# Attention products over all 128 rows, with scores one chunk ahead, in a two-layer convolution / mLSTM kernel

## The chip, the core and the metric

The kernel runs on one core of one Trainium2 chip. The metric is the device time of one execution in microseconds (us); less is better. The engines are TensorE (PE, with its weight loads as PEld), VectorE (DVE), ScalarE (ACT), GpSimd (POOL) and SyncE (SP), which here issues the DMAs.

## The reference

Two layers of a small diffusion backbone on 1024 latent and 256 context tokens of width 1024: first a gated short convolution, then a bidirectional mLSTM with eight heads, each followed by a squared-ReLU MLP. All is float32. The change lies in the mLSTM. For a head (q and k 64 wide, v 128 wide), a direction and a chunk of 128 tokens the reference computes

```python
logd = b[..., :, None] - b[..., None, :] + ic[..., None, :]
logd = jnp.where(tri, logd, -jnp.inf)
s = jnp.einsum('bhtd,bhsd->bhts', qc, kc) * jnp.exp(logd - m_t[..., None])
num = jnp.einsum('bhts,bhsv->bhtv', s, vc) + w_inter[..., None] * jnp.einsum('bhtd,bhdv->bhtv', qc, c_mat)
den = jnp.sum(s, axis=-1) + w_inter * jnp.einsum('bhtd,bhd->bht', qc, n_vec)
out = num / jnp.maximum(jnp.abs(den), jnp.exp(-m_t))[..., None]
...
c_new = a[..., None, None] * c_mat + jnp.einsum('bhsd,bhsv->bhdv', kc * wk[..., None], vc)
```

and adds the outputs of the forward and of the backward direction. The states c_mat and n_vec at each chunk's start are carried over the chunks.

## The kernel before

The layers follow each other on the one core. In the mLSTM the heads go in four pairs (0 to 3); two heads of 64 lie one above the other in the 128 partitions. For a pair the kernel projects k, v and q (`psk`, `psv`, `psq`, products of float32r with 128 rows), then comes `states` and then `attend` for each of its two heads.

`states` transposes k chunk by chunk (`pk`), weighs it (`kk`), multiplies it with V, and puts the forward state of each of ten steps in partitions 0 to 63 of `st[hh]`, the backward one in 64 to 127 (L977 on ACT, L978 on DVE). Eight recurrences per head on DVE (L982) carry the states on.

`attend` takes eight chunks of 128 latent tokens. First `qw`: the weights w of both directions are fetched into the two halves of the partitions (L993) and multiplied with the head's q (L994). Then for each chunk c:

- `Dm`, a tile for two chunks and both directions, is fetched every second chunk (L1002), gets the triangular mask added on DVE (L1004) and is put through the exponential on ACT (L1009); three buffers.
- the scores `po` (L1011): 64 rows of kT against 64 rows of qT, those of the head;
- `pm` (L1015, DVE): the scores times both directions' exponentials;
- for each direction d a product of `pm` with V over 128 rows (L1019) and, added to it in PSUM, one of 64 rows of `qw` with 64 rows of the state (L1020). The column 128 of the 129 is the denominator; each direction has a PSUM bank of its own;
- absolute values on ACT (L1026), maximum and reciprocal on DVE (L1027, L1028), the forward output scaled on ACT (L1030), the backward one scaled and added on DVE (L1031), and the sum of squares on ACT (L1032).

The outputs `hb` of a head (four buffers) wait for `out_gate` (projection `pso`, sigmoid) and `read_out` (transposes `pth`), which stand after the next pair's psq.

The order on each engine is static. A scheduler makes it when the program is built: it follows priorities, and puts projections of the next pair (psk, psv; in pair 3 the pso of pairs 2 and 3) between the chunks. SP issues its DMAs in order too, and a DMA whose buffer is not yet free holds up those behind it.

## Time and profile before

| | us |
|---|---|
| three runs | 2639.1, 2613.77, 2613.24 |
| median of these | 2613.77 |
| profiled execution | 2626.18 |
| its span, first to last instruction | 2624.4 |

| engine | busy us | share of the span |
|---|---|---|
| PE | 2549.2 | 97% |
| DVE | 1634.4 | 62% |
| ACT | 1149.1 | 44% |
| POOL | 98.8 | 4% |

Busy time is the time in which an instruction of the engine runs. Instructions overlap, so that an engine's pace is read from the starts of successive ones, not from their lengths. A float32 product stands in the trace as two records. `64*128` in a row is rows times columns of the array that the weights fill. The granted clock is that of TensorE, as a share of 2.4 GHz.

### The profile page before, as it was taken

Reading aid. Unit: us, or ns where it says so; the run is one execution under the profiler, and the core shown is the slowest. Engines: PE = TensorE matmul, PEld = TensorE weight load, DVE = VectorE, ACT = ScalarE, POOL = GpSimd, SP = SyncE. Lnnn points to the kernel's source line nnn. Section 1 sums busy time; section 2 is a strip of 40 time slices with the busy share of each in tenths; the row PEclk is TensorE's granted clock in tenths of the full one; section 3 lists DMA queues with packets and bytes.
Section 4 is the critical chain, followed back from the end, with each engine's and each line's share of the span. In section 5 each row is a group of like instructions: output and inputs, shape, how many; then the busy total and the mean of one; then the engine's idle time right before and its main releaser. Section 6 shows DMA issues by size and latency. Waiting matters only on the chain.

```text
span 2624.4 us, 38836 instructions
## 1 busy us (share of the span) xinstructions
PE 2549.2 (97%) x14520; PEld 2227.5 (85%) x14520; DVE 1634.4 (62%) x3036; ACT 1149.1 (44%) x2545; POOL 98.8 (4%) x223
## 2 busy tenths in 40 slices
PE   8999999979999999999999999999998999999998
PEld 5888887879999998888878888787878999988887
DVE  5677885677676664455764653526567777754565
ACT  6311113555445453334654534335455555554443
POOL 1000000100000000000120000000010000000010
PEclk9999999989999999999999999979999999999999
DMA  8456653436665675556741322221435777676665
GB/s 290 129 183 191 209 178 114 147 122 228 224 231 210 221 253 169 171 155 195 232 147 53 70 70 68 61 53 37 150 108 199 260 241 261 230 254 190 184 224 189
DMA packets 229631, 452.77 MB, mean 173 GB/s; under 512 B 17738, under 2 KB 109178, under 8 KB 229442
## 3 DMA queue, kind: packets, MB, share of 16 engines
q1 hardware_dynamic: 229442, 450.29, 53.1%
q8 instruction: 114, 1.87, 0.3%
q14 instruction: 75, 0.61, 0.1%
HBM read 324.68 MB, written 125.33 MB: 171 GB/s over the span
## 4 chain that ended last, share of the span: by engine, by line
PE 54%; issue 30%; DMA 7%; DVE 6%; ACT 2%; POOL 1%; SPq 0%; DVEq 0%; POOLq 0%; ACTq 0%
PE psd L528 11%; PE op L371 5%; PE psv L853 4%; PE psZ L429 4%; PE psW L429 4%; PE psX L429 4%; PE pso L129 3%; DMA mraw<-in_mod_w_dram 3%; PE psc L129 2%; PE psY L429 2%; DMA Dm<-nm_d 2%; PE psu L129 2%; PE psb L129 2%; PE po L1020 1%; DVE macc L220 1%
## 5 line engine op out<-in xcount | busy, mean ns | idle before, releaser
L528 PE MATMUL psd<-w,hp 128*128 128x512 f32 x3024 | 705.0, 395 | 0.0
L528 PEld LDWEIGHTS psd<-w,hp 128*128 128x128 f32 x3024 | 568.9, 188 | 132.2 <-DVE p L548 0.2
L523 DVE TENSOR_TENSOR hp<-hr,hp 128x512 fp32r<-128x512 f32 (+1 forms) x226 | 169.3, 751 | 255.1 <-ACT hp L522 254.8
L522 ACT CAST hp<-hr 128x512 fp32r<-128x512 f32 (+1 forms) x226 | 151.2, 669 | 325.8 <-PE psd L528 295.6
L123 DVE TENSOR_TENSOR w<-raw,w 128x512 fp32r<-128x512 f32 x384 | 261.1, 684 | 37.2 <-ACT w L122 36.8
L122 ACT CAST w<-raw 128x512 fp32r<-128x512 f32 x384 | 236.4, 617 | 95.9 <-DMA raw<-in_w_dram 31.4
L429 PE MATMUL psX<-A,w 128*128 128x256 f32 (+1 forms) x1536 | 233.2, 300 | 5.0 <-ACT st L444 3.7
L429 PE MATMUL psZ<-A,w 128*128 128x256 f32 (+1 forms) x1536 | 230.8, 298 | 1.0 <-DVE st L448 1.0
L429 PE MATMUL psW<-A,w 128*128 128x256 f32 (+1 forms) x1536 | 228.1, 296 | 0.0
L429 PEld LDWEIGHTS psX<-A,w 128*128 128x128 f32 x1536 | 216.2, 191 | 6.4 <-ACT st L444 4.0
L429 PEld LDWEIGHTS psZ<-A,w 128*128 128x128 f32 x1536 | 215.2, 190 | 1.4 <-DVE st L448 1.4
L429 PEld LDWEIGHTS psW<-A,w 128*128 128x128 f32 x1536 | 213.2, 189 | 0.0
L371 PE MATMUL op<-w,zs 128*128 128x512 f32 x864 | 203.3, 394 | 1.7 <-ACT zs L365 1.7
L459 ACT ACTIVATE st<-st 128x256 f32<-128x256 f32 (+1 forms) x192 | 85.3, 444 | 247.7 <-DVE st L450 182.3
L371 PEld LDWEIGHTS op<-w,zs 128*128 128x128 f32 x864 | 160.9, 188 | 37.6 <-ACT zs L365 2.4
L220 DVE SCALAR_TENSOR_TENSOR macc<-mraw,sil,macc 128x1024 f32<-128x1024 f32 x112 | 140.5, 1280 | 38.7 <-DMA mraw<-in_mod_w_dram 38.4
L109 ACT CAST w<-raw 128x1024 fp32r<-128x1024 f32 (+1 forms) x73 | 75.3, 1039 | 161.2 <-PE psc L129 60.9
L853 PE MATMUL psv<-w,hT 128*128 128x256 f32 (+1 forms) x960 | 144.8, 305 | 0.9 <-ACT val L270 0.9
L853 PEld LDWEIGHTS psv<-w,hT 128*128 128x128 f32 x960 | 130.5, 201 | 7.6 <-issue 2.0
L429 PE MATMUL psY<-A,w 128*128 128x256 f32 (+1 forms) x768 | 121.7, 305 | 13.2 <-ACT w L122 11.6
L110 DVE TENSOR_TENSOR w<-raw,w 128x1024 fp32r<-128x1024 f32 (+1 forms) x73 | 87.6, 1208 | 69.3 <-ACT w L109 68.2
L429 PEld LDWEIGHTS psY<-A,w 128*128 128x128 f32 x768 | 111.3, 195 | 15.7 <-ACT w L122 12.4
(238 smaller groups left out, 3462.2 us busy)
## 6 DMA issues: line engine op xcount, KB each, us to landing
hid_d<-st SPq DMA_DIRECT2D x48, 896.0 KB, 5.3
mraw<-in_mod_w_dram SPq DMA_DIRECT2D x80, 512.0 KB, 3.9
hr<-hid_d SPq DMA_DIRECT2D x104, 320.0 KB, 4.0
raw<-in_w_dram SPq DMA_DIRECT2D x64, 512.0 KB, 4.2
rw<-in_w_dram SPq DMA_DIRECT2D x64, 512.0 KB, 5.8
raw<-t_d SPq DMA_DIRECT2D x128, 256.0 KB, 3.1
hr<-hid_d SPq DMA_DIRECT2D x122, 256.0 KB, 2.7
raw<-in_w_dram SPq DMA_DIRECT2D x96, 256.0 KB, 3.2
```

The source lines that it names most:

```text
L110: nc.vector.tensor_sub(w[1], src, w[0].bitcast(F32))
L122: nc.scalar.copy(w[:, 0], src)
L123: nc.vector.tensor_sub(w[:, 1], src, w[:, 0].bitcast(F32))
L129: nc.tensor.matmul(ps, w[a][:, k * P : (k + 1) * P], hold["hT"][:, k, b, t0 : t0 + n], start=(k == 0 and i == 0), stop=(k == KD - 1 and i ...
L220: nc.vector.scalar_tensor_tensor(ac[v], raw, s, ac[v], ALU.mult, ALU.add)
L371: nc.tensor.matmul(ps[h], zs[:, a, k, :], ws[k][b][:, h * 512 : (h + 1) * 512], start=(k == 0 and i == 0), stop=(k == KD - 1 and i == 2),)
L429: nc.tensor.matmul(ps, w[i][:, a, k * P : (k + 1) * P], A[:, PIECE[i], b, k, :], start=(first and k == 0 and j == 0), stop=(k == 3 and j = ...
L459: nc.scalar.activation(c, c, AF.Relu)
L522: nc.scalar.copy(h[:, 0], r)
L523: nc.vector.tensor_sub(h[:, 1], r, h[:, 0].bitcast(F32))
L528: nc.tensor.matmul(ps, h[:, a, o : o + P], w[:, b], start=(first and j == 0), stop=(last and j == 2))
L853: nc.tensor.matmul(ps[:, 0 : self.g], hold["hT"][:, k, a_, t * P : (t + 1) * P], self.wv[k // self.per][b_][:, k % self.per * self.g : (k ...
```

## The change

- `qz`, one tile for all pairs, takes the place of each pair's `qT`: for head 0 of the pair q stands in partitions 0 to 63 and zeros in 64 to 127, for head 1 the other way round. ACT copies each psq in two halves. The scores are then a product over all 128 rows of kT.
- `sts`, two state tiles made once, hold for each step the forward state over zeros, and beside it (index 1) zeros over the backward state. The recurrences (now L994) run over both, 258 columns instead of 129. The state product then takes all 128 rows of `qw`, the weighted q of both directions as one operand; the zeros take away the other direction.
- The zeros are written once, by memsets on POOL (L809, L810, L967, L968).
- Both directions' outputs lie in the bank of the scores (columns 128 to 385), so that one ACT instruction takes both absolute values.
- `front(c)` (Dm, exponentials, scores, pm) and `back(c)` (the other products and the output) are apart, and `front(c + 1)` is written ahead of `back(c)`.
- `Dm` and `hb` have two buffers instead of three and four; in pair 3 `hb` takes the buffers of kT and V.

```diff
@@ -803,6 +803,11 @@
         flcol = K1.tile([P, 8, 2, 8], F32, name="flcol")
         adb = K1.tile([P, HEADS, NT], F32, name="adb")
         mask = K1.tile([P, 2, P], F32, name="mask")
+
+        lower, upper = slice(0, 64), slice(64, P)
+        qz = K1.tile([P, 2, SEQ], F32, name="qz")
+        nc.gpsimd.memset(qz[upper, 0], 0.0)
+        nc.gpsimd.memset(qz[lower, 1], 0.0)
         nc.gpsimd.memset(mask, 0.0)
         NEG = -1e30
         nc.gpsimd.affine_select(mask[:, 0], mask[:, 0], pattern=[[1, P]], compare_op=ALU.is_ge, fill=NEG, base=0, channel_multiplier=-1)
@@ -830,7 +835,6 @@
                 self.j = j
                 self.kT = pr.tile([P, TOK], F32, tag="kT", name="kT")
                 self.V = pr.tile([P, NT, 2, 129], F32, tag="V", name="V")
-                self.qT = pr.tile([P, SEQ], F32, tag="qT", name="qT")
                 nc.gpsimd.memset(self.V[:, :, :, 128:129], 1.0)
                 self.g, self.per = (GP, 3) if j == 0 else (256, 4)
                 with tc.high_priority(offset=HP if j == 0 else 0):
@@ -866,7 +870,10 @@
                 for t0, n in groups:
                     ps = tp.tile([P, 512], F32, tag="tp", name="psq")
                     mm_feat(ps[:, 0:n], w, t0, n)
-                    nc.scalar.activation(self.qT[:, t0 - CTX : t0 - CTX + n], ps[:, 0:n], AF.Identity, scale=0.125)
+                    for hh, r in enumerate((lower, upper)):
+                        nc.scalar.activation(
+                            qz[r, hh, t0 - CTX : t0 - CTX + n], ps[r, 0:n], AF.Identity, scale=0.125
+                        )
 
         XG = ((256, 512), (768, 512))
         pair = Pair(0)
@@ -954,9 +961,14 @@
 
         hp = s1.enter_context(pool("head", bufs=2, side="right"))
 
+
+        sts = [hp.tile([P, NT, 2, 129], F32, name=f"st{i}", bufs=1) for i in range(2)]
+        for t in sts:
+            nc.gpsimd.memset(t[upper, :, 0], 0.0)
+            nc.gpsimd.memset(t[lower, :, 1], 0.0)
+
         def states(pair):
             j = pair.j
-            st = [hp.tile([P, NT, 129], F32, tag="st", name="st") for _ in range(2)]
             for c in range(NT):
                 pk = acc.tile([P, 512], F32, tag="acc", name="pk")
                 nc.tensor.transpose(pk[:, 0:P], pair.kT[:, c * P : (c + 1) * P], ident)
@@ -974,62 +986,76 @@
                         pk[:, o : o + 129], kk[:, hh].rearrange("p d q -> p (d q)"), pair.V[:, c, hh],
                         start=True, stop=True,
                     )
-                    nc.scalar.copy(st[hh][0:64, c], pk[0:64, o : o + 129])
-                    nc.vector.tensor_copy(st[hh][64:128, sb], pk[64:128, o : o + 129])
+                    nc.scalar.copy(sts[hh][lower, c, 0], pk[lower, o : o + 129])
+                    nc.vector.tensor_copy(sts[hh][upper, sb, 1], pk[upper, o : o + 129])
             for hh in range(2):
                 h = 2 * j + hh
                 for s_ in range(1, NT - 1):
                     nc.vector.scalar_tensor_tensor(
-                        st[hh][:, s_], st[hh][:, s_ - 1], adb[:, h, s_ : s_ + 1], st[hh][:, s_], ALU.mult, ALU.add
+                        sts[hh][:, s_], sts[hh][:, s_ - 1], adb[:, h, s_ : s_ + 1], sts[hh][:, s_], ALU.mult, ALU.add
                     )
-            return st
-
-        def attend(pair, hh, st):
+
+        def attend(pair, hh):
             h = 2 * pair.j + hh
-            pb = hh * 64
-            kT, qT, V = pair.kT, pair.qT, pair.V
+            kT, V, st = pair.kT, pair.V, sts[hh]
             qw = hp.tile([P, SEQ], F32, tag="qw", name="qw")
-            for d in range(2):
-                nc.sync.dma_start(qw[d * 64 : d * 64 + 64], w_d[d, h].partition_broadcast(64))
-                nc.vector.tensor_mul(qw[d * 64 : d * 64 + 64], qw[d * 64 : d * 64 + 64], qT[pb : pb + 64])
-            hb = hp.tile([P, 8, P], F32, tag="hb", name="hb", bufs=4)
+            for d, r in enumerate((lower, upper)):
+                nc.sync.dma_start(qw[r], w_d[d, h].partition_broadcast(64))
+                nc.vector.tensor_mul(qw[r], qw[r], qz[hh * 64 : hh * 64 + 64, hh])
+            if pair.j < HEADS // 2 - 1:
+                hb = hp.tile([P, 8, P], F32, tag="hb", name="hb")
+            else:
+                hb = pr.tile([P, 8, P], F32, tag="V" if hh else "kT", name="hb")
             ssq = small.tile([P, 8], F32, tag="ssq", name="ssq", bufs=4)
-            for c in range(8):
-                cs = slice(c * P, (c + 1) * P)
-                g = c + NCT
+            Dm = {}
+
+            def front(c):
+
                 if c % 2 == 0:
-                    Dm = hp.tile([P, 2, 2 * P], F32, tag="Dm", name="Dm", bufs=3)
-                    nc.sync.dma_start(Dm, nm_d[:, h, c * P : (c + 2) * P].partition_broadcast(P))
+                    D2 = hp.tile([P, 2, 2 * P], F32, tag="Dm", name="Dm")
+                    nc.sync.dma_start(D2, nm_d[:, h, c * P : (c + 2) * P].partition_broadcast(P))
                     for d in range(2):
                         nc.vector.tensor_add(
-                            ch(Dm[:, d]), ch(Dm[:, d]), mask[:, d].unsqueeze(1).broadcast_to([P, 2, P])
+                            ch(D2[:, d]), ch(D2[:, d]), mask[:, d].unsqueeze(1).broadcast_to([P, 2, P])
                         )
-                Dc = Dm[:, :, (c % 2) * P : (c % 2 + 1) * P]
+                    Dm[c], Dm[c + 1] = D2[:, :, 0:P], D2[:, :, P : 2 * P]
+                Dc = Dm[c]
                 for d in range(2):
                     nc.scalar.activation(Dc[:, d], Dc[:, d], AF.Exp, bias=acol[:, c, d, h : h + 1])
                 po = acc.tile([P, 512], F32, tag="acc", name="po")
+                g = c + NCT
                 nc.tensor.matmul(
-                    po[:, 0:P], kT[pb : pb + 64, g * P : (g + 1) * P], qT[pb : pb + 64, cs], start=True, stop=True
+                    po[:, 0:P], kT[:, g * P : (g + 1) * P], qz[:, hh, c * P : (c + 1) * P], start=True, stop=True
                 )
                 pm = hp.tile([P, 2, P], F32, tag="pm", name="pm")
                 nc.vector.tensor_mul(pm, po[:, 0:P].unsqueeze(1).broadcast_to([P, 2, P]), Dc)
-                o = (po[:, 128:257], acc.tile([P, 512], F32, tag="acc", name="po1")[:, 0:129])
+                return po, pm
+
+            def back(c, po, pm):
+                g = c + NCT
+                o = po[:, 128:386].rearrange("p (d v) -> p d v", d=2)
                 steps = (g - 1, NT - g)
                 for d in range(2):
-                    nc.tensor.matmul(o[d], pm[:, d], V[:, g, hh], start=True, stop=False)
+                    nc.tensor.matmul(o[:, d], pm[:, d], V[:, g, hh], start=True, stop=False)
                     nc.tensor.matmul(
-                        o[d], qw[d * 64 : d * 64 + 64, cs], st[hh][d * 64 : d * 64 + 64, steps[d]],
-                        start=False, stop=True,
+                        o[:, d], qw[:, c * P : (c + 1) * P], st[:, steps[d], d], start=False, stop=True
                     )
                 dn = small.tile([P, 2], F32, tag="dn", name="dn")
-                for d in range(2):
-                    nc.scalar.activation(dn[:, d : d + 1], o[d][:, 128:129], AF.Abs)
+                nc.scalar.activation(dn, o[:, :, 128], AF.Abs)
                 nc.vector.tensor_max(dn, dn, flcol[:, c, :, h])
                 nc.vector.reciprocal(dn, dn)
                 h1 = hp.tile([P, P], F32, tag="h1", name="h1")
-                nc.scalar.activation(h1, o[0][:, 0:P], AF.Identity, scale=dn[:, 0:1])
-                nc.vector.scalar_tensor_tensor(hb[:, c], o[1][:, 0:P], dn[:, 1:2], h1, ALU.mult, ALU.add)
+                nc.scalar.activation(h1, o[:, 0, 0:P], AF.Identity, scale=dn[:, 0:1])
+                nc.vector.scalar_tensor_tensor(hb[:, c], o[:, 1, 0:P], dn[:, 1:2], h1, ALU.mult, ALU.add)
                 nc.scalar.activation(h1, hb[:, c], AF.Square, accum_out=ssq[:, c : c + 1])
+
+            nxt_ = front(0)
+            for c in range(8):
+                cur = nxt_
+                if c < 7:
+                    nxt_ = front(c + 1)
+                back(c, *cur)
+
             def out_gate():
                 r = rstd_of(ssq, 8, 1.0 / P)
                 for i in range(0, 8, 4):
@@ -1070,8 +1096,8 @@
                 for og, ro in fin:
                     ro(og())
                 fin = []
-            st = states(pair)
-            fin += [attend(pair, hh, st) for hh in range(2)]
+            states(pair)
+            fin += [attend(pair, hh) for hh in range(2)]
         for og, ro in fin[:2]:
             ro(og())
         fin = fin[2:]
```

Two places show how the scheduled order moves. The first is TensorE in pair 1, late in its chunks; po are the chunks' products (scores L1011 before and L1027 after, with V L1019 and L1039, with the states L1020 and L1040), psv the filler. Before:

```order
L1019 MATMUL po<-V,pm 128x129
L1020 MATMUL po<-st,qw 128x129
L1019 MATMUL po_14209<-V,pm 128x129
L1020 MATMUL po_14209<-st,qw 128x129
L1011 MATMUL po<-qT,kT 128x128
L853 MATMUL psv<-w_14418,hT 128x256
L853 MATMUL psv<-w_14419,hT 128x256
L853 MATMUL psv<-w_14418,hT 128x256 x2
L853 MATMUL psv<-w_14419,hT 128x256
L1019 MATMUL po<-V,pm 128x129
L1020 MATMUL po<-st,qw 128x129
L1019 MATMUL po_14240<-V,pm 128x129
```

After:

```order
L1039 MATMUL po<-V,pm 128x129
L1040 MATMUL po<-st_12950,qw 128x129
L1039 MATMUL po<-V,pm 128x129
L1040 MATMUL po<-st_12950,qw 128x129
L1027 MATMUL po<-qz,kT 128x128 x2
L857 MATMUL psv<-w_14366,hT 128x256
L857 MATMUL psv<-w_14367,hT 128x256
L857 MATMUL psv<-w_14366,hT 128x256
L857 MATMUL psv<-w_14360,hT 128x256
L857 MATMUL psv<-w_14361,hT 128x256
L857 MATMUL psv<-w_14360,hT 128x256
L1027 MATMUL po<-qz,kT 128x128
```

Before, a chunk is four products of alternating rows, then the score of the next chunk, then some seven psv. After, the products of two or more chunks stand together, and two scores ahead of them; over a pair fewer psv stand between the chunks, and behind the last chunk stand 55, 197 and 197 psv in pairs 0 to 2 (28, 154 and 154 before) and 94 pso in pair 3 (71 before).

The second place is DVE in pair 1, with buffer numbers: each Dm is one load (Dm_14179, Dm_14230, Dm_14274, Dm_14318 follow each other before, Dm_14090, Dm_14130, Dm_14189 after), L1004 and L1018 are the masks, L1015 and L1031 the score multiplies. Before:

```order
L1015 TENSOR_TENSOR pm_14207<-po_14205,Dm_14179 128x256
L1028 RECIPROCAL dn_14194<-dn_14194 128x2
L1031 SCALAR_TENSOR_TENSOR hb_14045<-po1_14189,dn_14194,h1_14199 128x128
L1015 TENSOR_TENSOR pm_14238<-po_14236,Dm_14230 128x256
L1027 TENSOR_TENSOR dn_14214<-dn_14214,flcol_12235 128x2
L1028 RECIPROCAL dn_14214<-dn_14214 128x2
L1031 SCALAR_TENSOR_TENSOR hb_14045<-po1_14209,dn_14214,h1_14219 128x128
L1004 TENSOR_TENSOR Dm_14318<-Dm_14318,mask_12237 128x256 x2
L1027 TENSOR_TENSOR dn_14245<-dn_14245,flcol_12235 128x2
L1015 TENSOR_TENSOR pm_14258<-po_14256,Dm_14230 128x256
```

After:

```order
L1031 TENSOR_TENSOR pm_14116<-po_14114,Dm_14090 128x256
L1049 SCALAR_TENSOR_TENSOR hb_14020<-po_14074,dn_14104,h1_14108 128x128
L1031 TENSOR_TENSOR pm_14138<-po_14136,Dm_14130 128x256
L1045 TENSOR_TENSOR dn_14122<-dn_14122,flcol_12235 128x2
L1046 RECIPROCAL dn_14122<-dn_14122 128x2
L1031 TENSOR_TENSOR pm_14156<-po_14154,Dm_14130 128x256
L1049 SCALAR_TENSOR_TENSOR hb_14020<-po_14096,dn_14122,h1_14126 128x128
L1045 TENSOR_TENSOR dn_14144<-dn_14144,flcol_12235 128x2
L1046 RECIPROCAL dn_14144<-dn_14144 128x2
L1018 TENSOR_TENSOR Dm_14189<-Dm_14189,mask_12237 128x256 x2
```

Before, the load of Dm_14318 waits for pm_14207 (third load back), and its mask stands ahead of pm_14258, for which the next load waits. After, the load of Dm_14189 waits for pm_14116 (second load back), and its mask stands behind both pm of the load between, pm_14138 and pm_14156, for the second of which the following load waits.

## Rows read from the trace of the kernel before

**Rows 1.** Stretches: from:to us, length, busy us (instructions) by engine, granted clock, DMA.

```profile
1476.00:1508.00 32.00, 30.02 (x185) 23.97 (x184) 15.16 (x58) 18.75 (x82) 1.99 (x3) 1.00 0.31 62
...
1576.00:1612.00 36.00, 34.59 (x197) 27.72 (x195) 16.98 (x61) 19.59 (x87) 2.13 (x2) 0.91 0.33 70
...
1696.00:1745.00 49.00, 47.45 (x196) 38.16 (x195) 17.41 (x60) 19.58 (x86) 1.97 (x2) 0.62 0.22 54
```

**Rows 2.** Chain that ended last, in order of time: start us, us, what.

```profile
1438.81 1.26 PE pk L962 x5
...
1511.09 11.16 PE psq L129 x48
...
1546.30 0.44 PE pk L962 x4
...
1612.51 18.46 PE psv L853 x154
1630.98 11.16 PE psq L129 x48
...
1666.20 0.44 PE pk L962 x4
...
1745.59 18.47 PE psv L853 x154
...
1862.31 7.89 PE op L371 x34
```

**Rows 3.** Timeline of PE: start us, us, line, shapes; a chunk of each head.

```profile
1473.85 0.38 PE L1019 MATMUL po<-V,pm 128*128 128x129 f32 x2
...
1475.00 0.37 PE L1020 MATMUL po<-st,qw 64*128 64x129 f32 x1
1475.01 0.37 PE L1011 MATMUL po<-qT,kT 64*128 64x128 f32 x1
...
1475.42 0.39 PE L853 MATMUL psv<-w,hT 128*128 128x256 f32 x1
...
1484.79 0.38 PE L1019 MATMUL po<-V,pm 128*128 128x129 f32 x2
1485.11 0.49 PE L1020 MATMUL po<-st,qw 64*128 64x129 f32 x2
...
1486.27 0.38 PE L1011 MATMUL po<-qT,kT 64*128 64x128 f32 x2
1486.58 1.09 PE L853 MATMUL psv<-w,hT 128*128 128x256 f32 x7
```

**Rows 4.** Timeline of PE in pair 1: 128-row products beside their like.

```profile
1562.38 0.61 PE L1019 MATMUL po<-V,pm 128*128 128x129 f32 x4
1562.82 0.44 PE L973 MATMUL pk<-V,kk 128*128 128x129 f32 x2
```

**Rows 5.** Timeline of DVE, and three pieces of the chain, in pair 1.

```profile
1584.40 0.76 DVE L1004 TENSOR_TENSOR Dm<-Dm,mask 128x256 f32<-128x256 f32 x2 [1.78 <-DMA Dm<-nm_d]
...
1590.56 0.76 DVE L1004 TENSOR_TENSOR Dm<-Dm,mask 128x256 f32<-128x256 f32 x2 [1.40 <-DMA Dm<-nm_d]
...
1572.79 0.42 DVE pm L1015
...
1579.20 5.18 DMA Dm<-nm_d
```

**Rows 6.** Timeline of SP (pair 1), a group on ACT, timeline of DVE (pair 0).

```profile
1561.91 17.66 SPq L1002 DMA_DIRECT2D Dm<-nm_d  x3
...
L1009 ACT ACTIVATE Dm<-Dm,acol 128x128 f32<-128x128 f32 x24 | 8.3, 392 | 2.3 <-DVE Dm L1004 2.2
...
1462.17 2.73 DVE L982 SCALAR_TENSOR_TENSOR st<-st,adb 128x129 f32<-128x129 f32 x10
```

**Rows 7.** Timeline of POOL, and the tile qT: ns min/median/max.

```profile
1363.99 1.17 POOL L813 MEMSET gcol<- 128x1280 f32 x1 [0.85 <-DVE tt L294]
...
L869 ACT ACTIVATE qT<-psq x8: 577/594/599, 1414.0 to 1776.0; 128x512 f32<-128x512 f32 x8
```

## The prediction

> **What bounds the kernel now.** I read first the busy shares by stretch [rows 1], because the change lies only in the attention part of the mLSTM layer (1438.8 to 1862.3 us of the span; 16 chunks of scores and outputs for each of four head pairs). There TensorE is the engine that is nearly always busy: it stands still for 1.98 us of 32, 1.41 of 36 and 1.55 of 49. The reason is that projections of the next pair (psk, psv, pso) were put between the chunks as filler. Second I read the chain [rows 2]: after each pair's last chunk comes a tail of projections alone (154 psv in 18.5 us, 0.12 us each, then 48 psq in 11.2, 0.232 each). So a pair ends when TensorE has done all its work, or when the chunks' own loop is through and the tail after it.
>
> Third, the same engine's timeline [rows 3], chunk by chunk. A product of 128x129 is two records. A chunk of head 1 has five products and takes from 1484.79 to 1486.58, that is 1.79 us; one of head 0 from 1473.85 to 1475.42, 1.57 us. Where a 128-row product stands beside its like, two take 0.44 us, 0.22 each [rows 4]; alternating with 64-row ones (64\*128 in the row) they take 0.32 to 0.42. That extra is the price of the change of rows.
>
> Last, VectorE [rows 5]: the mask is added to a freshly loaded tile Dm (two chunks) at 1584.40 and 1590.56, each time after waiting 1.78 and 1.40 us for its load. A load takes 5.2 us. In DVE's order before, the mask of load k+3 stands ahead of the score multiply (pm) that frees the next buffer, so that loads follow each other one by one despite three buffers: load 5.2, mask 0.8, pm 0.4, about 6.4 us for two chunks. TensorE's 3.5 us of products plus filler just fits into that. Both bounds lie close together, and this decides the sum.
>
> A fourth thing: the clock. In pair 2 the same program as in pair 1 has a granted clock of 0.62 in the mean instead of 0.91 [rows 1], that is, long at 1.2 instead of 2.4 GHz, and from its first pk to its psv tail it takes 79.4 us instead of 66.2 [rows 2]: 13.2 us more. It fell while TensorE was working all the time on 64- and 128-row products in turn.
>
> **The change, part by part.** (a) All products take 128 rows: five products at 0.22 make 1.1 us a chunk, against a mean of 1.68 (1.57 and 1.79). That frees 0.58 x 64 = 37 us of TensorE, if nothing else moves. What I do not see is a 128-row product with half its operand zero; I take the price of the full one, 0.22 [rows 4], to which it is nearest in shape. The bounds are 0.21, what each of the two overlapping products of head 0 takes (1475.00 to 1475.42 [rows 3]), and 0.32, the cheapest product that stands beside a change of rows; at 0.32 a chunk would cost 1.6 and nothing would be gained.
>
> At one place a rule speaks against it. In head 0 the last product of a chunk and the score of the next start at 1475.00 and 1475.01 [rows 3]: they lie on different halves of the rows and run together, and head 0's chunk is 0.22 us shorter for it. The Trainium skill (TensorE: Matmul & The Clock Gate, Part 3, "The mechanism") says that small products on distinct row groups run concurrently, so that padding gives something up. The trace agrees for this neighbour pair. By that rule alone the change would lose 0.22 x 32 = 7 us; the 1.57 above already contains this overlap, and the gain of 0.58 is net of it.
>
> (b) Scores one chunk ahead, Dm with two buffers instead of three. The static order moves (order rows of the section on the change). On DVE both pm of load k+1 now stand ahead of the mask of load k+2: two loads are in flight together. One round is then load 5.2, mask 0.8, four exponentials 1.4 (0.35 each [rows 6]), pm 0.4: 7.7 us, but for two loads, four chunks: 1.9 us a chunk instead of 3.2. On TensorE the filler is packed differently: four chunks come with little between, and the psv tails grow from 154 to 197 (28 to 55 in pair 0, and in pair 3 from 71 pso to 94). So part of what TensorE gains is stood idle in the loop, waiting for loads.
>
> (c) The state recurrences on DVE now run over 258 columns instead of 129. Ten of them took 2.73 us [rows 6], 0.27 each. For 258 the bounds are 0.38 (half of the 0.76 of the two masks, 256 columns [rows 5]) and 0.54 (twice 0.27). I take 0.41, near the pm of 256 columns with its 0.42: 16 x 0.14 = 2.2 us more for each pair, in a stretch in which the first outputs wait for the last recurrence.
>
> **Pair 1, step by step.** The second pm of load 0 is done at 1561.9 (SP issues a load then [rows 6]); the states before it do not change. On DVE follow a pm, three copies (together 1.5) and 15 recurrences (6.2), then the second pm of load 1: 1569.8. The last recurrence, the first outputs with their scaling (about 3), the mask of load 3 (issued at 1569.8, landed at 1575.0), exponentials and pm bring load 2 to its second pm at about 1577.7. Two rounds of 7.7: load 6 is through at 1593.1. The last chunk's pm stands behind the mask of the next pair's first load, issued at that time: + 5.2 + 0.8 + 0.4, and four products 0.9: 1600.4. Tail 197 x 0.12 = 23.6: 1624.0, against 1631.0 now: **-7.0**. TensorE's own work would allow 1631.0 - 16 x 0.58 - 1.4 - 0.09 x 36 (the clock of 0.91) = 1617.1, so some 7 us of new idle time appear.
>
> Pair 2 has the same order: **-7.0**. Pair 0: its ten recurrences end at 1464.9 now [rows 6]; 2.2 later, with a pm, load 0 is through at 1467.5, load 2 (landed 1472.7; mask, pm, and a weighting of q, an estimate of 3 together) at about 1475.7, load 3's second pm behind load 4's mask (1481.6), in steps of 7.7 for loads 5 and 7 to 1497, output 1498, 55 psv 6.6: 1504.6 against 1511.1: **-6.5**. Pair 3: the mask of load 2 stands ahead of twelve recurrences, which stay behind its landing (issued at the first pm of head 6, by the distance in pair 0 some 20 us after that pair's start, 1795; landed 1800, then 5 for the recurrences and 2 for outputs and pm): load 2 is through only at about 1807, loads 4 and 6 at 1817 and 1827, the last outputs at 1834, then 94 pso (21.8) and 18 transposes (2.0): 1857.8 against 1862.3: **-4.5**. Sum: -25.0.
>
> (d) At nothing: the memsets of qz and of the two state tiles on POOL (each at most the 1.17 us of a larger one [rows 7]; POOL has nothing else to do there, and TensorE the psv of pair 1; without that cover the first chunk of pair 0 would come 4.7 us later). The second ACT instruction for each psq (8 x 0.6 us [rows 7]) is hidden by the 5.6 us that the next psq takes; ACT saves 64 of the 128 reads of the denominators. One output bank instead of two: ACT's first read waits for all four products, 0.4 us in a loop in which the load lasts longest. qz and the states in one copy: a pair's q is written after the last chunk before it, behind the psv tail of 18 us; without that it would wait up to one chunk.
>
> **Sum.** The profiled execution took 2626.18 us (span 2624.4 and 1.8 around it). The median of the runs, 2613.77, is 12.4 below; this is nearly the 13.2 us of the clock in pair 2. So 2626.2 - 13.2 - 25.0 = 2588.0: I predict 2588, 26 us or 1.0% below the median.
>
> **Rivals.** (1) Loads hide entirely, TensorE alone bounds: 2613 - 37 for the products - 5 to 10 for stalls and half clock now there = 2566 to 2571. For it: DMA queues are little used; against: masks standing ahead of pm in the order. (2) The clock stays at its lower level in one or two pairs, because TensorE now waits some 7 us in each: +13 each as in pair 2, 2601 with one, 2614 with two. For it: the clock fell twice in this part already [rows 1], and gaps get longer; against: products without row changes are denser, and a loop that waits for loads loses less to a slow TensorE. (3) Slower: the two buffers act as one, each load only after the last pm of the one before, 7.7 us for two chunks. Six loads after 1569.8 end at 1616.0, with output and tail 1640.5: 9.5 us more for each pair, 2613 + 38 = 2651. It decides from 6.1 us a load on, where a pair ends as now; I expect 5.0 (from 1569.8 to 1599.5 in six). Against it the order of DVE. (4) The extra on the 64-row products comes from something other than the change of rows; then the lost overlap and the longer recurrences count alone: 2613 + 7 + 4 x 2.2 = 2629. That is the rule on row groups above, taken alone.
>
> **How the numbers follow.** Main case 0.50 (own range 2576 to 2600: some 24 rounds, each up to half a microsecond longer or shorter), rival 1 0.21, rival 2 0.19, rival 3 0.06, rival 4 0.04. Range for 8 in 10: from 2564 (rival 1's lower end, less 2 to 3 for products of 0.21) to 2607, between one and two pairs at the low clock. A change of 1% (26 us) is about what a measurement can tell from none. Faster by over 1% (below 2587.6): 0.25 of the main case, all of rival 1, and 0.02 of rival 2, where the loop hides the slow clock: 0.48. Within: 0.25 + 0.17 + 0.04 = 0.46. Slower: 0.06.
>
> **What would show it.** In the profile after: products of 0.22 us without longer neighbours, about 1.1 us per chunk; DVE waiting for Dm about once per four chunks, 2 to 3 us; recurrences of 0.4; psv tails of 197 that start some 39 us after the second pm of load 0; pairs 1 and 2 some 7 us shorter than pair 1 now. The prediction is wrong if a 128-row product beside zeros costs over 0.3 us, if the mask waits come once per two chunks, or if the granted clock of the attention stretches lies below 0.8.

## The result, and the profile after

Over nine runs each the kernel takes 2593.73 us after the change (2591.92 to 2597.03) and 2616.85 before (2612.24 to 2654.64). The ratio of the means is 0.9898, with a 95% interval of 0.9872 to 0.9925; the one slow run before, 2654.64, is left out of it. The profiled execution took 2592.09 us, its span is 2590.3 (2626.18 and 2624.4 before).

The chain of waits after, in order of time (start us, us, what), answers [rows 2]:

```profile
1438.33 1.26 PE pk L974 x5
...
1506.34 11.14 PE psq L129 x48
...
1541.54 0.44 PE pk L974 x4
...
1558.80 4.87 DVE st L994 x12
...
1600.03 17.37 PE psv L857 x144
1617.40 11.15 PE psq L129 x48
...
1652.65 0.44 PE pk L974 x4
...
1704.01 23.65 PE psv L857 x197
1727.66 11.14 PE psq L129 x48
1738.80 0.66 PE pk L974 x6
...
1798.43 21.85 PE pso L129 x94
1820.29 1.32 PE pth L1077 x12
...
1825.67 1.22 DVE w L110
1826.89 1.08 DVE zs L366 x2
...
1828.01 7.00 PE op L371 x22
```

A pair lasts from its first pk to the next psq, pair 3 to op. From these rows and [rows 2] (where a psv tail ends, psq begins; pair 3 of before begins after psq, at 1745.59 + 18.47 + 11.1 = 1775.2):

| pair | before us | after us | difference | predicted |
|---|---|---|---|---|
| 0 | 72.3 | 68.0 | -4.3 | -6.5 |
| 1 | 84.7 | 75.9 | -8.8 | -7.0 |
| 2 | 97.9 | 75.0 | -22.9 | -20.2 (7.0 and 13.2 of the clock) |
| 3 | 87.1 | 89.2 | +2.1 | -4.5 |

Their sum is -33.9 of the 34.1 us by which the span is shorter; 1862.31 to the end of the span before, and 1828.01 to its end after, are both 762 us. The medians differ by 23.1 only: the profiled execution before, 9 us above its median, is one in which the clock fell in pair 2.

The stretches answer [rows 1] (from:to us, length, busy us and instructions by engine PE, PEld, DVE, ACT, POOL, granted clock, DMA):

```profile
1476.00:1506.00 30.00, 23.14 (x180) 22.33 (x179) 16.07 (x59) 17.37 (x76) 3.83 (x5) 0.94 0.41 85
1574.00:1600.00 26.00, 20.93 (x167) 19.51 (x166) 14.67 (x54) 16.16 (x73) 2.67 (x5) 1.00 0.48 114
```

The first stretch lies in pair 0, the second in pair 1. In pair 1 the clock is 1.00 where it was 0.91. But TensorE now stands still for a fifth or more of the chunk loop: 6.9 of 30 us and 5.1 of 26. What it waits for is on the timeline of PE and in its waits from 1436 to 1830 (us in total, times, longest):

```profile
1577.53 0.49 PE L1027 MATMUL po<-qz,kT 128*128 128x128 f32 x2 [1.67 <-DVE hb L1049]
```

```profile
PE po L1027 <- DVE hb L1049: 16.8, 12, 2.3
PE po L1039 <- DVE pm L1031: 5.5, 6, 1.7
PE op L371 <- ACT zs L365: 2.7, 1, 2.7
...
PE op L371 <- DVE zs L366: 2.1, 1, 2.1
```

Mostly a score waits for `hb`. It needs a PSUM bank, and a bank is free only when the output of an earlier chunk has been read out of it. That reading is late on DVE, as its timeline shows (idle time before an instruction, and what ended it, in brackets):

```profile
1575.31 0.76 DVE L1018 TENSOR_TENSOR Dm<-Dm,mask 128x256 f32<-128x256 f32 x2 [2.12 <-DMA Dm<-nm_d]
1575.99 1.22 DVE L110 TENSOR_TENSOR w<-raw,w 128x1024 fp32r<-128x1024 f32 x1
1577.12 0.35 DVE L1049 SCALAR_TENSOR_TENSOR hb<-po,dn,h 128x128 f32<-128x128 f32 x1
...
1584.33 0.76 DVE L1018 TENSOR_TENSOR Dm<-Dm,mask 128x256 f32<-128x256 f32 x2 [0.87 <-DMA Dm<-nm_d]
...
1587.88 0.76 DVE L1018 TENSOR_TENSOR Dm<-Dm,mask 128x256 f32<-128x256 f32 x2 [0.62 <-DMA Dm<-nm_d]
...
1591.42 0.42 DVE L1018 TENSOR_TENSOR Dm<-Dm,mask 128x256 f32<-128x256 f32 x1 [1.34 <-DMA Dm<-nm_d]
```

A mask waits for its load until 1575.31, and `hb` stands behind it in DVE's order, and behind a weight split of 1.22 us (L110). What `hb` reads, ACT had ready at 1574.50. Such waits for loads are not new on DVE: it had 19 of them before, 28.4 us in all, and has 23 now, 38.3 us. New is that TensorE, sooner done with its products, stands still meanwhile (rows64 below, with the slower products, hardly does). The products themselves now run at one pace (timeline of PE, pair 1; eight products, 0.22 us from start to start after the first):

```profile
1586.50 0.49 PE L1039 MATMUL po<-V,pm 128*128 128x129 f32 x2
1586.83 0.39 PE L1040 MATMUL po<-st,qw 128*128 128x129 f32 x2
...
1588.16 0.39 PE L1040 MATMUL po<-st,qw 128*128 128x129 f32 x2
1588.31 0.97 PE L857 MATMUL psv<-w,hT 128*128 128x256 f32 x6
```

### The profile page after: what moved, and what is told of

The parts are those of the page before. It is cut to its first block, busy times and chain, and to the rows that moved or that the text cites. A ratio compares the mean times of both kernels' runs of the same rounds, so it can differ in the third digit from the quotient of the medians.

```text
span 2590.3 us, 38783 instructions
## 1 busy us (share of the span) xinstructions
PE 2489.9 (96%) x14520; PEld 2202.5 (85%) x14520; DVE 1640.9 (63%) x3036; ACT 1139.0 (44%) x2489; POOL 104.8 (4%) x229
## 4 chain that ended last, share of the span: by engine, by line
PE 53%; issue 30%; DVE 7%; DMA 6%; ACT 2%; POOL 2%; SPq 0%; DVEq 0%; POOLq 0%; ACTq 0%
PE psd L528 11%; PE op L371 5%; PE psZ L429 4%; PE psW L429 4%; PE psX L429 4%; PE psv L857 3%; PE psc L129 3%; PE pso L129 3%; PE psb L129 3%; PE psu L129 3%; DMA Dm<-nm_d 3%; PE psY L429 2%; DMA mraw<-in_mod_w_dram 2%; PE psq L129 1%; POOL rstd L242 1%
## 5 line engine op out<-in xcount | busy, mean ns | idle before, releaser
L110 DVE TENSOR_TENSOR w<-raw,w 128x1024 fp32r<-128x1024 f32 (+1 forms) x73 | 87.8, 1210 | 80.1 <-ACT w L109 79.0
L857 PE MATMUL psv<-w,hT 128*128 128x256 f32 (+1 forms) x960 | 133.8, 293 | 1.1 <-ACT val L270 0.9
L857 PEld LDWEIGHTS psv<-w,hT 128*128 128x128 f32 x960 | 123.7, 192 | 1.9 <-ACT val L270 1.2
L429 PEld LDWEIGHTS psY<-A,w 128*128 128x128 f32 x768 | 111.2, 195 | 15.2 <-ACT w L122 12.4
```

Source lines behind the costliest of these rows:

```text
L110: nc.vector.tensor_sub(w[1], src, w[0].bitcast(F32))
L429: nc.tensor.matmul(ps, w[i][:, a, k * P : (k + 1) * P], A[:, PIECE[i], b, k, :], start=(first and k == 0 and j == 0), stop=(k == 3 and j = ...
L857: nc.tensor.matmul(ps[:, 0 : self.g], hold["hT"][:, k, a_, t * P : (t + 1) * P], self.wv[k // self.per][b_][:, k % self.per * self.g : (k ...
```

## The experiments

All start from the changed kernel. Its time for comparison is 2593.7 us. The kernel before, run beside each group, took 2636.5 (15 runs), 2624.1 (7), 2635.5 (7) and 2620.1 us (11) in the median, between 2609.9 and 2667.2; so each experiment's own median is compared. The changed kernel was not run again beside them, and the profiles differ outside the pairs too: the first pk starts anywhere from 1435.3 to 1442.5 us. A difference of 5 us or less counts here only where the lengths of the pairs bear it out.

**rows64: the 64-row products back.**

```diff
-                    po[:, 0:P], kT[:, g * P : (g + 1) * P], qz[:, hh, c * P : (c + 1) * P], start=True, stop=True
+                    po[:, 0:P], kT[hh * 64 : hh * 64 + 64, g * P : (g + 1) * P], qz[hh * 64 : hh * 64 + 64, hh, c * P : (c + 1) * P],
...
-                        o[:, d], qw[:, c * P : (c + 1) * P], st[:, steps[d], d], start=False, stop=True
+                        o[d], qw[d * 64 : d * 64 + 64, c * P : (c + 1) * P], st[d * 64 : d * 64 + 64, steps[d], d],
```

> The changed kernel with 64-row scores and state products again (zeros unread), outputs of the two directions in two PSUM banks; all else as changed. Theory (price of the change of rows): 0.58 us more for each of 64 chunks, 37 us of TensorE, of which the 26 us that it stands still in the chunk loops take in some half: 2605 to 2622, most likely 2612, with a chunk of 1.6 to 1.8 us in the trace. Rival (the extra came from something other than the row change): the overlap of neighbours on different rows returns 7 us of TensorE and nothing else changes, 2585 to 2592. If the granted clock falls in one pair, 13 more.

Measured: 2613.25 us (2609.48 to 2621.55), 19.5 above the changed kernel, as the theory has it. The timeline of PE in pair 1 shows both sides of the bargain:

```profile
1579.76 0.37 PE L1041 MATMUL po<-st,qw 64*128 64x129 f32 x1
1579.76 0.37 PE L1027 MATMUL po<-qz,kT 64*128 64x128 f32 x1
...
1587.39 0.49 PE L1041 MATMUL po<-st,qw 64*128 64x129 f32 x2
1587.81 0.49 PE L1040 MATMUL po<-V,pm 128*128 128x129 f32 x2
...
1588.64 0.85 PE L857 MATMUL psv<-w,hT 128*128 128x256 f32 x5
```

Neighbours on different halves of the rows start together (1579.76 and 1579.76), but where 64 and 128 rows alternate each product takes 0.42 us from start to start instead of 0.22. A change of rows thus costs 0.2 us. The Trainium skill (TensorEngine Tiling (Array Packing), Key Properties) says that changing the tiling mode drains TensorE; the 0.2 us of the trace fit that, and the page has no price. In pair 1, at a clock of 1.00 in both kernels, TensorE is busy for 80.5 us instead of 69.8: 0.67 more for each of 16 chunks. It stands still 1.2 us at most in each of pairs 0 to 2 here: the price takes the place of the waits.

The profiled execution shows a second price. The stretches of pairs 0 and 1:

```profile
1438.40:1516.00 77.60, 77.39 (x452) 65.56 (x452) 48.38 (x152) 35.70 (x150) 6.18 (x7) 0.84 0.32 76
1551.10:1632.00 80.90, 80.51 (x525) 67.76 (x524) 43.39 (x145) 36.95 (x149) 3.84 (x5) 1.00 0.24 60
```

In pair 0 the granted clock is 0.84, with TensorE idle for 0.2 us of 77.6, as it was 0.62 in pair 2 of before [rows 1]. In pairs 1 to 3 the same products run at 1.00, so the 64-row products alone do not bring the clock down; what does stays open.

**seq: the chunks written one after the other.**

```diff
-            nxt_ = front(0)
             for c in range(8):
-                cur = nxt_
-                if c < 7:
-                    nxt_ = front(c + 1)
-                back(c, *cur)
+                back(c, *front(c))
```

> The changed kernel with front(c) and back(c) written one after the other, so scores are not written a chunk ahead. Theory: the scheduler reorders by readiness anyway and its order is nearly that of the changed kernel (tails of 184 psv instead of 197, masks two loads ahead as before); 2588 to 2596, no difference. Rival (scores ahead is what lets two loads fly together): one load for two chunks in 6.4 us instead of 7.7 for four, 5 to 10 us more for each pair, 2612 to 2630.

Measured: 2591.95 us (2586.50 to 2594.55): no difference that counts, as the theory has it. Writing the scores one chunk ahead does nothing that shows, since the scheduler moves instructions by readiness anyway. PE waits as long for `hb` as in the changed kernel (16.4 us, 12 times).

**fill: the next pair's projections between the chunks.**

```diff
                 back(c, *cur)
+                for f in (fill or {}).get((hh, c), ()):
+                    f()
...
+                todo += [lambda t=t, p=nxt: p.v([t]) for t in all_tiles]
```

> The changed kernel with the next pair's psk and psv written between the chunks, one tile of psv (24 products) after each chunk or two, for pairs 0 to 2; nothing is left as a tail. Theory (TensorE waits in the loop only because the filler was left for the tail): of the 20 us that it stands still in the loops of pairs 0 to 2 some 14 to 18 go, 2574 to 2579. Rival (loads and VectorE's order set the pace of the chunks in any case): the loop gets as much longer as the tail gets shorter and waits stay, 2588 to 2596.

Measured: 2596.86 us (2594.66 to 2598.72): the rival, 3 us slower even. The 3 us do not lie in the loops: the four pairs together take 308.5 us against 308.1, and the first pk starts 4.2 us later. Pair 1 takes 76.4 us, 75.9 with the tail. Timeline of PE, then of DVE:

```profile
1595.13 0.80 PE L1039 MATMUL po<-V,pm 128*128 128x129 f32 x2 [4.12 <-DVE pm L1031]
```

```profile
1593.44 1.29 DVE L1064 TENSOR_TENSOR hb<-hb,rstd 128x512 f32<-128x512 f32 x2 [2.47 <-POOL rstd L242]
1594.66 0.75 DVE L1031 TENSOR_TENSOR pm<-po,Dm 128x256 f32<-128x256 f32 x2
```

A product stands still for 4.12 us, and the psv placed behind it cannot pass it. What holds it is DVE's order again, this time the scaling of `hb` that waits for `rstd`. Where the filler lies does not matter while DVE holds the products up.

**rows64_fill: both.** The diffs are those of rows64 and fill.

> rows64 and fill together: 64-row products where TensorE hardly waits, so that nothing hides their price. Theory (price of the change of rows, 0.58 us a chunk): 37 us above fill, less the few that pair 3's waits hide, so 30 to 37 above it, about 2610 if fill takes 2576. Rival (no such price): 7 us below fill, 2569.

Measured: 2628.92 us (2622.07 to 2638.83), 32 above fill, in the expected 30 to 37, but not for the reason given. TensorE was to wait little in fill; it stands still for 26.9 us in fill's four pairs, and for 6.0 here, so part of the price hides in waits as in rows64. And part of the 32 is the clock: in the profiled execution, the slowest of ten, it is 0.90, 0.96, 0.96 and 0.89 in the four pairs (0.92, 0.96, 0.98 and 1.00 in fill). The four runs with a mean clock of 0.986 or 0.987, at least that of fill (0.984), take 2622.07 to 2627.22 us, 25 to 30 above it.

**noload: no loads of Dm.**

```diff
-                    nc.sync.dma_start(D2, nm_d[:, h, c * P : (c + 2) * P].partition_broadcast(P))
...
-                            ch(D2[:, d]), ch(D2[:, d]), mask[:, d].unsqueeze(1).broadcast_to([P, 2, P])
+                            ch(D2[:, d]), mask[:, d].unsqueeze(1).broadcast_to([P, 2, P]), mask[:, d].unsqueeze(1).broadcast_to([P, 2, P])
...
-                    nc.scalar.activation(Dc[:, d], Dc[:, d], AF.Exp, bias=acol[:, c, d, h : h + 1])
+                    nc.scalar.activation(Dc[:, d], Dc[:, d], AF.Exp)
```

> The changed kernel without the loads of Dm: VectorE makes the tile from the mask alone (same two instructions a tile) and the exponential has no bias, so the decay weights are left out. Theory (waiting for loads, directly or through VectorE's queue, is what TensorE stands still for in the chunk loops, some 20 of 26 us): 2570 to 2578, with the wait of scores for hb gone too. Rival (other waits take their place: recurrences, the outputs' scaling): 2584 to 2592.

Measured: 2556.98 us (2554.51 to 2560.91), 36.8 less, twice the expected. PE's waits from 1436 to 1790, all that are left in the loops, and the chain in pair 1:

```profile
PE po L1026 <- DVE hb L1048: 1.3, 1, 1.3
PE po L1038 <- DVE pm L1030: 1.0, 1, 1.0
```

```profile
1567.62 28.48 PE psv L857 x240
```

The tail is longest here, 240 psv, and it costs nothing: TensorE never waits in pairs 1 and 2. So the loads, and what stands behind them, are the cause of nearly all waits of the changed kernel. Of the 37.6 us by which the span is shorter, 24 are waits (26.5 over the four pairs in the changed kernel, 2.5 here). TensorE's busy time is 9 us less, which I can assign only in part (the clock is 0.96 instead of 0.94 in pair 0, 1.00 instead of 0.98 in pair 3); 3 us lie ahead of the first pk and 1 behind op. The exponential without its bias takes ACT 0.31 us instead of 0.39; its share was not measured by itself.

**dm1: loads of one chunk.**

```diff
-                    D2 = hp.tile([P, 2, 2 * P], F32, tag="Dm", name="Dm")
-                    nc.sync.dma_start(D2, nm_d[:, h, c * P : (c + 2) * P].partition_broadcast(P))
+                Dc = hp.tile([P, 2, P], F32, tag="Dm", name="Dm", bufs=4)
+                nc.sync.dma_start(Dc, nm_d[:, h, c * P : (c + 1) * P].partition_broadcast(P))
```

> The changed kernel with Dm loaded for one chunk at a time into four buffers of half the size (the same memory), one mask instruction a chunk. Theory (a buffer's round of load, mask, exponentials and pm of two chunks sets the loop's pace): the rounds get shorter, half of the 20 us of waits go, 2578 to 2586. Rival (a load's time is mostly latency, twice as many loads cost as much as they bring; and 219 psv instead of 197 are left for the tail): 2589 to 2596.

Measured: 2588.47 us (2587.09 to 2592.74), 5 less; between the two, next to the rival. The pairs bear it out: together they take 4 us less. Over the four pairs a load of 128 KB lands after 4.6 us in the median, one of 256 KB in the changed kernel after 4.7 (in pair 1 4.7 and 4.4): halving a load does not bring it noticeably earlier.

**dm1x6_fill: six such buffers, and fill.**

```diff
-        sts = [hp.tile([P, NT, 2, 129], F32, name=f"st{i}", bufs=1) for i in range(2)]
+        sts = [hp.tile([P, NT - 1, 2, 129], F32, name=f"st{i}", bufs=1) for i in range(2)]
...
+                Dc = hp.tile([P, 2, P], F32, tag="Dm", name="Dm", bufs=6)
```

> dm1 with six buffers, the memory coming from a tenth state slot that nothing reads (its copies go too), and the next pair's projections between the chunks as in fill. Theory (fill brought nothing because two buffers then held the first chunks back, while the last ones were bound by TensorE): with loads far ahead TensorE stands still little in pairs 0 to 2, 2570 to 2580. Rival (what holds the first chunks back is the recurrences and not the loads): 2588 to 2597 as fill.

Measured: 2599.55 us (2596.80 to 2601.61): slower than without both. Timeline of PE, then of DVE, then one piece of the chain, in pair 1:

```profile
1584.42 0.80 PE L1035 MATMUL po<-V,pm 128*128 128x129 f32 x2 [4.63 <-DVE pm L1027]
```

```profile
1566.36 0.42 DVE L1027 TENSOR_TENSOR pm<-po,Dm 128x256 f32<-128x256 f32 x1
...
1568.04 0.42 DVE L1027 TENSOR_TENSOR pm<-po,Dm 128x256 f32<-128x256 f32 x1 [0.21 <-PE po L1023]
1572.28 0.43 DVE L1018 TENSOR_TENSOR Dm<-Dm,mask 128x256 f32<-128x256 f32 x1 [3.82 <-DMA Dm<-nm_d]
...
1582.74 1.29 DVE L1060 TENSOR_TENSOR hb<-hb,rstd 128x512 f32<-128x512 f32 x2 [2.48 <-POOL rstd L242]
1583.95 0.75 DVE L1027 TENSOR_TENSOR pm<-po,Dm 128x256 f32<-128x256 f32 x2
```

```profile
1566.90 5.36 DMA Dm<-nm_d
```

In pair 0, whose first loads find all buffers free, the two edits together do help: it takes 60.5 us instead of 68.0 (68.8 with fill alone). Pairs 1 and 2 take 81.9 and 82.1 instead of 75.9 and 75.0, and the rows show why. The pm at 1566.36 frees a buffer, and the load into it starts at 1566.90. Its mask stands in DVE's order only one pm later, at 1572.28, though with six buffers it serves a chunk far ahead, so DVE waits 3.82 us for it. There are 40 such waits, 67.3 us in all, against 23 and 38.3 us in the changed kernel. The long wait of PE at 1584.42 is again one for the scaling behind `rstd`. A mask placed later in the order was not tried.

**qwhb: pair 3's hb over its own qw.**

```diff
-                hb = pr.tile([P, 8, P], F32, tag="V" if hh else "kT", name="hb")
+                hb = qw.rearrange("p (c v) -> p c v", v=P)
```

> The changed kernel with pair 3's hb written over its own qw (chunk by chunk, after the products that read it) instead of into kT's and V's buffers. Theory (zs of the out projection lies in the memory of those buffers, so it must wait for the last transposes, and TensorE stands still 4.8 us before op): zs of the first six heads is made before the last gates, op follows the transposes at once, 2586 to 2588. Rival (the three weight splits behind the last gates are what op waits for): no change, 2590 to 2593.

Measured: 2585.63 us (2579.67 to 2587.19), 8.1 less, and the lowest median of the versions that compute all. Pair 3 takes 81.3 us instead of 89.2, which is this difference. (The ratio to before, 0.9862 with an interval of 0.9830 to 0.9893, does not rank the versions: fill has 0.9860, since before varies.) Timeline of DVE, then of PE, at the end of pair 3:

```profile
1807.58 0.96 DVE L366 TENSOR_TENSOR zs<-zt,zs 128x768 fp32r<-128x768 f32 x1 [3.58 <-ACT zs L365]
...
1819.83 2.73 DVE L1079 SCALAR_TENSOR_TENSOR sg<-pth,cols,sg 128x512 f32<-128x512 f32 x4 [8.32 <-PE pth L1077]
```

```profile
1819.20 1.91 PE L1077 MATMUL pth<-ident,qw 128*128 128x128 f32 x16
1820.86 11.09 PE L371 MATMUL op<-w,zs 128*128 128x512 f32 x47
```

The operand `zs` of the out projection is now made 12 us before the last gates, and op follows the transposes at once. In the changed kernel it was made after them and after three weight splits (1826.89 in the chain above), and op ran freely only from 1828.01. The cause is memory: `zs` takes over that of kT and V, where `hb` still lay.

**poolmask_qwhb: the mask on GpSimd.**

```diff
-                        nc.vector.tensor_add(
+                        nc.gpsimd.tensor_add(
```

> qwhb with the mask added on GpSimd instead of VectorE. Theory (a mask that waits for its load blocks the outputs and pm behind it on VectorE, and that is most of what the loads cost): the waits for loads leave VectorE's queue, and of the 35 us between the changed kernel and the one without loads some 15 come back on top of qwhb's 2585.6: 2566 to 2576. Rival (the load itself is late, whoever adds the mask; GpSimd also makes rstd, which now stands behind masks that wait): 2583 to 2592.

Measured: 2599.26 us (2598.68 to 2600.24), 13.6 above qwhb: worse than the rival. GpSimd takes 1.40 us for the two masks of a tile in the row below, where DVE took 0.76 (0.85 for one in the mean, against 0.42), and `rstd` stands behind them. Timeline of POOL in pair 1, and a wait of DVE (1436 to 1836):

```profile
1575.53 1.40 POOL L1018 TENSOR_TENSOR Dm<-Dm,mask 128x256 f32<-128x256 f32 x2 [3.40 <-DMA Dm<-nm_d]
```

```profile
DVE hb L1062 <- POOL rstd L242: 21.7, 6, 5.4
```

The wait has only changed its queue: DVE now stands up to 5.4 us behind `rstd` (2.5 in the changed kernel, 15.2 in all).

**dm1px6_qwhb: the same with six small buffers.** The diffs are those of poolmask_qwhb and of dm1x6_fill without fill.

> poolmask_qwhb with Dm loaded chunk by chunk into six buffers of half the size (memory from the state slot that nothing reads). Theory (with the mask off VectorE only the latency of a buffer's round is left, and six small buffers hide it): 5 to 10 us below poolmask_qwhb, 2558 to 2570. Rival (SyncE issues its loads in order behind those for weights and qw, so more buffers do not bring them earlier): within 3 us of poolmask_qwhb.

Measured: 2591.86 us (2588.93 to 2597.13). It is 7.4 below poolmask_qwhb, as the theory has it in size, but far above the 2558 to 2570 expected, since poolmask_qwhb lies 13.6 above qwhb. It ends 6 above qwhb: nothing is gained in all.

**rec129: the recurrences halved.**

```diff
-                        sts[hh][:, s_], sts[hh][:, s_ - 1], adb[:, h, s_ : s_ + 1], sts[hh][:, s_], ALU.mult, ALU.add
+                        sts[hh][:, s_, 0], sts[hh][:, s_ - 1, 0], adb[:, h, s_ : s_ + 1], sts[hh][:, s_, 0], ALU.mult, ALU.add
```

> The changed kernel with the recurrences over the forward 129 columns alone (the backward states are not carried on). Theory (the recurrences stand before the first outputs of each pair, 16 x 0.14 = 2.2 us more in each): 2583 to 2588. Rival (the first outputs wait for the load of Dm in any case): 2590 to 2594.

Measured: 2590.53 us (2589.06 to 2598.71): the rival. One recurrence lasts 0.349 us instead of 0.482 (its whole length; neighbours overlap), but pairs 0 to 2 take 68.6, 76.7 and 76.5 us instead of 68.0, 75.9 and 75.0: what the recurrences give back is waited for loads. Pair 3 is 1.8 us shorter.

**combined: dm1 and qwhb, and hb scaled on GpSimd.**

```diff
-                    nc.vector.tensor_mul(
+                    nc.gpsimd.tensor_mul(
                         hb[:, i : i + 4], hb[:, i : i + 4], r[:, i : i + 4].unsqueeze(2).broadcast_to([P, 4, P])
```

> The changed kernel with pair 3's hb over qw (qwhb), Dm loaded chunk by chunk into four small buffers (dm1), mask still on VectorE, and the scaling of hb by rstd on GpSimd instead of VectorE. Theory (gains of different places add: 7 from the end of pair 3, 4 from shorter loads, and 2 to 8 from VectorE no longer standing behind rstd in its queue, 10 to 15 us of waits in all): 2572 to 2582. Rival (only the end of pair 3 adds, since in the loop the next wait takes the place of each removed one and the tails grow to 229 psv): 2583 to 2588.

Measured: 2590.24 us (2587.86 to 2597.29): above both ranges and 4.6 above qwhb alone. DVE's waits behind `rstd` are gone, and those for loads have grown (DVE, then PE, 1436 to 1826):

```profile
DVE Dm L1016 <- DMA Dm<-nm_d: 43.3, 39, 2.7
```

```profile
PE po L1033 <- DVE pm L1025: 17.6, 14, 2.0
```

In the changed kernel these were 38.3 and 5.5 us. Pair 3 keeps its gain (81.4 us up to its last transposes, and op follows), but pairs 1 and 2 take 77.5 and 79.0 us: the next wait has taken the place of each removed one. GpSimd takes 1.05 us for one scaling where DVE took 0.69; what this costs was not separated.

## Why the prediction was right

The time, 2593.7, lies in the range and 5.7 above the 2588 forecast, in the main case's own range. The profiled execution, 2592.1, is 4.1 above it. Step by step:

- **(a) The price of the rows: right.** 0.22 us a product beside zeros, so 1.1 a chunk. With 64 rows again TensorE works 0.67 us more a chunk in pair 1 (0.58 taken); rows64 and rows64_fill, 19.5 and 32 us slower, show what is left of that behind waits, and hold a part that is the clock's. The rule of the Trainium skill that spoke against the change (TensorE: Matmul & The Clock Gate, Part 3) holds for its neighbour pair, as the starts at 1579.76 show, and it is outweighed.
- **(b) New waits for loads: the size nearly right, the way wrong.** The prediction had 7 us of new idle time per pair. From the first pk to psq, or to the last transposes in pair 3, TensorE stands still for 8.3, 6.1, 5.7 and 6.4 us against 2.0, 1.5, 1.6 and 0.6 before: 4 to 6 more in each, and noload shows that loads cause it. The pace of the loads came out too: from the mask of 1575.31 to that of 1591.42, the next pair's first, four loads pass, 4.0 us each, with 3.85 predicted. Luck has a part in it: the 5.2 us for a load came from one row, the median of the 32 loads is 4.7 before and after, and a round of 7.2 instead of 7.7 would have given 3.6. The masks' waits are shorter and more frequent than foreseen: 23 for 32 loads, one in 2.8 chunks, 1.7 us in the mean, where the prediction had one in four chunks, and took one in two as a sign against itself. The path was wrong: not pm but mostly the PSUM bank that `hb` frees is what TensorE waits for, 16.8 us against 5.5. I had looked at what the load's own chunk needs, and not at what stands behind the mask on DVE. That `front` is written ahead plays no part (seq). Whether two buffers instead of three matter was not tried by itself.
- **(c) The recurrences: duration right, place wrong.** 0.41 us each (4.87 for 12), as taken. But the 2.2 us per pair that I charged for them are hidden behind loads: rec129 gives back 3 us of 8.8 at most, and nothing in pairs 0 to 2.
- **(d) At nothing: true but for one part.** Memsets and ACT's copies of q appear nowhere in the chain. But that `hb` lies in the buffers of kT and V in pair 3 has no term in the sum at all: I did not ask who takes over that memory. It costs some 6.4 us: pair 3's last transposes end at 1821.6, 82.8 us after the pair's start, where before the whole pair took 87.1 (4.3 less; predicted 4.5), and then op waits until 1828.0. This is the term that failed: +2.1 instead of -4.5, or 6.6 us, more than the 4.1 by which the profiled execution missed the forecast. qwhb shows it.
- **Pairs 0 to 2.** -4.3, -8.8 and -22.9 against -6.5, -7.0 and -20.2: -36.0 against -33.7. Errors of 2 to 3 us each way, which partly cancel, and the 2.3 us that remain hide part of pair 3's error. That the total came so close is partly luck.
- **The clock: right.** Rival 2 did not come: the granted clock is 1.00 in the loops of pairs 1 and 2, and the mean clock of all nine runs lies between 0.984 and 0.989. The kernel before has a low clock more often than its three runs had shown: beside the experiments its mean clock went from 0.963 to 0.991, and its medians from 2616.9 to 2636.5 hold this.

Rival 1 (TensorE alone, 2566 to 2571) was the right question: without loads the kernel takes 2557, and the loads are what stands between.

## What to carry to other kernels

A product beside zeros was worth it here because products of different numbers of rows alternated: count the changes of rows, not the multiplications. Before a wait is moved to an engine's queue or a filler is placed, list what stands behind the waiting instruction there; here five of the six attempts at the waits for loads that kept the loads (all but dm1) mostly moved them to the next queue or place. And where a tile takes other tiles' memory, ask who comes into that memory next.

## What the hardware showed beyond that

- A change between 64- and 128-row products costs TensorE 0.2 us each way (0.42 from start to start instead of 0.22), while two 64-row products on different halves start in the same 10 ns.
- With 64-row products between 128-row ones the granted clock fell in some stretches though TensorE hardly stood still: 0.84 over pair 0 of rows64 (idle for 0.2 us of 77.6), 0.62 in pair 2 of before [rows 1]. In pairs 1 to 3 of rows64 it was 1.00 with the same products. With 128 rows throughout it is 1.00 in the loops of pairs 1 and 2, and 0.94 in a stretch of pair 0 in which TensorE waits for 6.9 us of 30.
- A broadcast load of 128 KB lands hardly sooner than one of 256 KB (medians over four pairs 4.6 and 4.7 us; in pair 1 4.7 and 4.4).
- GpSimd adds two masks of 128x256 in 1.40 us, DVE in 0.76; over all 64 masks GpSimd takes 0.85 us for one, DVE 0.42.
